# Seven products for eight in one block of gate and up columns, spread through the feed-forward

## The chip, the cores and the metric

The kernel runs on one core of a Trainium2 chip. The metric is the device time of one execution in microseconds (us), as the median of the runs. TensorE (PE) multiplies, VectorE (DVE) and ScalarE (ACT) work on tiles in the on-chip memories SBUF and PSUM, GpSimd (POOL) and SyncE (SP) here mostly issue DMAs.

## The reference

One block of a Conformer kind on 256 rows of width 1024 (feed-forward, mixer, feed-forward), then two post-norm attention layers; all in float32. The change touches the two feed-forwards only:

```python
D_MODEL, SEQ, D_FF = 1024, 256, 2816

def swiglu_ffn(x, w_gate, w_up, w_down):
    return (jax.nn.silu(x @ w_gate) * (x @ w_up)) @ w_down

x = x + 0.5 * swiglu_ffn(rmsnorm(x, ffn1_norm[l]), ffn1_w_gate[l], ffn1_w_up[l], ffn1_w_down[l])
x = x + hybrid_mixer(...)
x = x + 0.5 * swiglu_ffn(rmsnorm(x, ffn2_norm[l]), ffn2_w_gate[l], ffn2_w_up[l], ffn2_w_down[l])
...
```

## The kernel before

A float32 product is made of three float32r matmuls: both factors are split into a rounded part and a rest (`hi`, `lo`), and `half` adds `xh*whi`, `xl*whi` and `xh*wlo` in one PSUM bank. The 256 rows are two tiles t = 0, 1 of 128, kept transposed in `xT[t]` as eight k tiles of 128.

**Units.** Weights come in units of 512 KB (`unit_list`, in the order of use): two k tiles by 512 columns, or, for the last 256 columns, four k tiles. `load` issues a unit's DMA on SP into one of four `raw` buffers; `prefetch` splits it, the rounding `whi` on ACT (L198), the rest `wlo` on DVE (L199), into one of eight pairs of buffers (`N_W`, `AHEAD`). So the split of a unit waits until TensorE has released the unit eight places earlier, and a DMA until the split four places earlier has read its buffer.

**A feed-forward** (`ffn`) goes through six blocks of columns, j = 0 to 4 of 512 and j = 5 of 256 (`FFN_CH`). For each there is a chunk of gate units and one of up units; a chunk is 4 units, which tile t = 0 uses in turn and then t = 1, 48 matmuls of 512 columns in all. The first gate chunk of the first feed-forward has 8 units of half the size, of which both tiles use each at once (`first_chunk`, `first_x`). A gate chunk's sums go through ACT (`th`) and DVE (`a`), an up chunk's through DVE (`h`, then its transpose `hb`). The block of h is then brought into the layout of the next product by a trip through device memory (`regroup`): four DMAs `d<-hb` and one `hd<-d`, all issued by POOL in its order. When `hd` is back, `put_h` splits it on ACT and DVE (`hh`, `hl`, L240 and L241) into `hT`. `put_h` is entered in the order a fixed time after the trip (`DUE["ffn_T"]`, 7 us of an estimated clock), and pinned there: what follows on ACT and DVE waits if `hd` is late. Before the down product's second last pair all that is due is entered (`drain`).

**The down product** takes 11 units (k tiles 0,1 to 20,21, in this order) for each half of the 1024 columns; a unit's 12 matmuls are six for each tile.

Each engine runs its instructions in order. The order is written by the program's loops and the estimated clock, and by a scheduler that may move unpinned instructions.

Of the kernel before, what the change touches and what calls it, by code (L numbers as in the profile page):

```python
# [45 lines left out]

def unit_list():
# [39 lines left out]
    "ffn_T": 7.0,  # L87
# [28 lines left out]
class Kern:  # L116
    def __init__(self, ctx, tc, A):
# [11 lines left out]
        self.raw, self.W = {}, {}  # L129
# [57 lines left out]
    def prefetch(self, splits):  # L187
        nc = self.nc
        for _ in range(splits):
            if self.n_split < min(len(UNITS), self.used + AHEAD):  # L190
                self.load(self.n_split)
                i = self.n_split
                raw = self.raw.pop(i)
                nk, w = UNITS[i][2], UNITS[i][4]
                hi = self.wp.tile([P, UK * 512], F32R, name="whi", tag="whi", bufs=N_W)
                lo = self.wp.tile([P, UK * 512], F32R, name="wlo", tag="wlo", bufs=N_W)
                m = nk * w
                nc.scalar.copy(hi[:, :m], raw[:, :m])  # L198
                nc.vector.tensor_sub(lo[:, :m], raw[:, :m], hi[:, :m].bitcast(F32))  # L199
                self.W[i] = (hi[:, :m].rearrange("p (k n) -> p k n", k=nk),  # L200
                             lo[:, :m].rearrange("p (k n) -> p k n", k=nk))
                self.n_split += 1
        self.load(self.n_split + N_RAW - 2)

    def load(self, upto):
        while self.n_dma <= min(upto, len(UNITS) - 1):
            i = self.n_dma
            m = UNITS[i][2] * UNITS[i][4]
            raw = self.wp.tile([P, UK * 512], F32, name="raw", tag="raw", bufs=N_RAW)
            w = self.A["w"]  # L210
            self.nc.sync.dma_start(out=raw[:, :m], in_=bass.AP(
                tensor=w.tensor, offset=w.offset + self.off[i], ap=[[m, P], [1, m]]))
            self.raw[i] = raw
            self.n_dma += 1

# [162 lines left out]
    def ffn(self, u, gain, next_gain):  # L378
        nc, tc = self.nc, self.tc
        with tc.tile_pool(name="ffn", bufs=1, reuse_waits="tile") as pool:  # L380
# [13 lines left out]
            for j, (c0, w) in enumerate(FFN_CH):  # L394
                nu = KT * w // (UK * 512)
                ng = KT if u == 0 else nu
                a = [None, None]
                gen = self.first_chunk(u, ng, gain) if u == 0 else \
                    self.chunk(u, ng, gain if j == 0 else None)
                for t, acc in gen:  # L400
                    if j == 0:
# [844 lines left out]
```

## Time and profile before

| | us |
|---|---|
| median of 3 runs (719.29, 720.04, 1176.42) | 720.04 |
| the profiled execution | 717.48 |
| its span, first to last instruction | 715.7 |
| TensorE busy | 701.6 |
| VectorE busy | 491.4 |
| ScalarE busy | 368.8 |

The profiled execution's own time is 1.8 us above its span. Busy TensorE time counts overlapping matmuls once; how fast it goes is read from the distance between matmuls. The first feed-forward lies at about 8 to 188 us, the second at about 283 to 463 us.

### The profile page before, as it was taken

How to read it: one execution, taken by the hardware profiler on the slowest of the kernel's cores; microseconds unless marked ns; L12 is line 12 of the kernel's file. 1: busy time of each engine (PE TensorE's matmuls, PEld its weight loads, DVE VectorE, ACT ScalarE, POOL GpSimd, SP SyncE). 2: the span in 40 equal slices, each digit the busy share in tenths (PEclk: the TensorE clock that was granted, in tenths of full speed). 3: DMA queues.
4: the chain of work that ended last, by engine and by line, in shares of the span. 5: the costliest groups of instructions: out<-in, count | busy, mean ns of one | idle time of the engine just before them, and what ended most of it. 6: DMA issues, size and time to landing. Idle time of an engine off the chain costs nothing.

```text
span 715.7 us, 9843 instructions
## 1 busy us (share of the span) xinstructions
PE 701.6 (98%) x3594; PEld 590.0 (82%) x3594; DVE 491.4 (69%) x790; ACT 368.8 (52%) x552; POOL 62.2 (9%) x90
## 2 busy tenths in 40 slices
PE   8999999999999999999999999999999999999995
PEld 6788888888888778888888888888898888778984
DVE  5867765576547878655865576555456968997965
ACT  6664544364546646353544364555465635675820
POOL 0101110200002001011110200000300001000001
PEclk9999999999999999999999999999999999999998
DMA  8888566876744435558656867555672527543501
GB/s 257 311 313 301 209 217 212 302 229 221 254 151 145 178 115 172 194 197 290 208 209 220 293 229 228 175 192 174 206 253 77 159 83 230 195 123 114 177 1 59
DMA packets 42305, 140.87 MB, mean 197 GB/s; under 512 B 5512, under 2 KB 6672, under 8 KB 42128
## 3 DMA queue, kind: packets, MB, share of 16 engines
q1 hardware_dynamic: 37728, 127.23, 52.9%
q0 software_dynamic: 4096, 12.60, 5.0%
q8 instruction: 28, 0.46, 0.3%
q10 hardware_dynamic: 432, 0.41, 0.2%
q14 instruction: 21, 0.17, 0.1%
HBM read 133.39 MB, written 6.82 MB: 196 GB/s over the span
## 4 chain that ended last, share of the span: by engine, by line
PE 89%; DVE 4%; DMA 4%; ACT 2%; issue 1%; POOL 0%; SPq 0%; DVEq 0%; ACTq 0%; POOLq 0%
PE mm L165 80%; PE sc L165 5%; PE tr L180 3%; DMA raw<-in_w 1%; DVE wlo L199 1%; DMA rope<-in_rope 1%; PE tr L165 1%; DMA xin<-in_xT 1%; ACT whi L198 1%; DMA gain<-in_gain 0%; ACT s L452 0%; DVE sel L994 0%; DVE sel L1003 0%; ACT xh L323 0%; DVE s L543 0%
## 5 line engine op out<-in xcount | busy, mean ns | idle before, releaser
L199 DVE TENSOR_TENSOR wlo<-raw,whi 128x1024 fp32r<-128x1024 f32 (+3 forms) x236 | 274.3, 1177 | 83.0 <-ACT whi L198 73.4
L198 ACT CAST whi<-raw 128x1024 fp32r<-128x1024 f32 (+3 forms) x236 | 235.2, 1013 | 126.9 <-PE mm L165 65.7
L165 PE MATMUL mm<-whi,xh 128*128 128x512 f32 (+3 forms) x760 | 288.4, 380 | 1.9 <-ACT whi L198 1.9
L165 PE MATMUL mm<-wlo,xh 128*128 128x512 f32 (+3 forms) x760 | 283.4, 373 | 0.1
L165 PE MATMUL mm<-whi,xl 128*128 128x512 f32 (+3 forms) x760 | 283.4, 373 | 0.0
L165 PEld LDWEIGHTS mm<-whi,xh 128*128 128x128 f32 x760 | 143.2, 188 | 25.7 <-ACT whi L198 3.7
L165 PEld LDWEIGHTS mm<-wlo,xh 128*128 128x128 f32 x760 | 143.1, 188 | 25.5 <-DVE wlo L199 1.9
L165 PEld LDWEIGHTS mm<-whi,xl 128*128 128x128 f32 x760 | 143.3, 189 | 22.4 <-DVE xl L249 0.2
L165 PE MATMUL mm<-whi,hh 128*128 128x512 f32 x176 | 68.7, 390 | 0.0
L165 PE MATMUL mm<-whi,hl 128*128 128x512 f32 x176 | 68.5, 389 | 0.0
L165 PE MATMUL mm<-wlo,hh 128*128 128x512 f32 x176 | 68.5, 389 | 0.0
L241 DVE TENSOR_TENSOR hl<-hd,hh 128x512 fp32r<-128x512 f32 (+1 forms) x24 | 14.5, 644 | 59.4 <-ACT hh L240 59.4
L240 ACT CAST hh<-hd 128x512 fp32r<-128x512 f32 (+1 forms) x24 | 12.9, 583 | 67.0 <-DMA hd<-d 67.0
L285 POOL DMA_DIRECT2D d<-hb x48 | 26.5, 558 | 149.2 <-DVE hb L420 149.1
L165 PEld LDWEIGHTS mm<-wlo,hh 128*128 128x128 f32 x176 | 33.0, 188 | 6.9
L165 PEld LDWEIGHTS mm<-whi,hh 128*128 128x128 f32 x176 | 33.1, 188 | 6.8
L165 PEld LDWEIGHTS mm<-whi,hl 128*128 128x128 f32 x176 | 33.1, 188 | 6.7
L407 ACT ACTIVATE th<-mm,hr 128x512 f32<-128x512 f32 (+1 forms) x24 | 15.5, 648 | 19.9 <-PE mm L165 18.8
L452 ACT ACTIVATE s<-s,nmax 128x128 f32<-128x128 f32 (+1 forms) x48 | 21.3, 446 | 7.0 <-DVE nmax L450 7.0
L299 POOL TENSOR_TENSOR rs<-ms,mhalf 128x1 f32<-128x1 f32 x10 | 6.5, 652 | 169.7 <-DVE ms L312 169.7
L299 POOL TENSOR_TENSOR lr<-ve,mhalf 128x1 f32<-128x1 f32 x4 | 4.0, 991 | 167.6 <-DVE ve L651 167.6
L409 DVE SCALAR_TENSOR_TENSOR a<-th,mm 128x512 f32<-128x512 f32 (+1 forms) x24 | 15.1, 628 | 5.0 <-ACT th L407 5.0
(219 smaller groups left out, 598.6 us busy)
## 6 DMA issues: line engine op xcount, KB each, us to landing
raw<-in_w SPq DMA_DIRECT2D x208, 512.0 KB, 4.6
d<-hb POOLq DMA_DIRECT2D x40, 128.0 KB, 4.7
hd<-d POOLq DMA_DIRECT2D x10, 512.0 KB, 6.5
raw<-in_w SPq DMA_DIRECT2D x12, 344.0 KB, 3.4
raw<-in_w SPq DMA_DIRECT2D x8, 372.0 KB, 3.5
raw<-in_w SPq DMA_DIRECT2D x8, 256.0 KB, 4.4
x<-in_x SPq DMA_DIRECT2D x2, 512.0 KB, 6.6
B<-in_bias SPq DMA_DIRECT2D x1, 1024.0 KB, 5.5
```

Source lines behind the costliest of these rows:

```text
L165: self.nc.tensor.matmul(out, a, b, start=start, stop=stop)
L180: self.nc.tensor.transpose(out, a, self.ident[:p, :p])
L198: nc.scalar.copy(hi[:, :m], raw[:, :m])
L199: nc.vector.tensor_sub(lo[:, :m], raw[:, :m], hi[:, :m].bitcast(F32))
L240: i = nc.scalar.copy(hi, src)
L241: j = nc.vector.tensor_sub(lo, src, hi.bitcast(F32))
L285: self.nc.gpsimd.dma_start(out=d[a].rearrange("b i m -> i b m"), in_=src[32 * a:32 * a + 32])
L299: self.nc.gpsimd.tensor_tensor(out, a, self.mhalf[:, 0:1].to_broadcast(list(a.shape)), op=ALU.pow)
L407: nc.scalar.activation(th[:, :w], acc[:, :w], AF.Tanh, scale=hr[t])
L409: nc.vector.scalar_tensor_tensor(a[t][:, :w], th[:, :w], 1.0, acc[:, :w], op0=ALU.add, op1=ALU.mult)
L452: nc.scalar.activation(s[:, h, :], s[:, h, :], AF.Exp, bias=m[:, h:h + 1], accum_out=l[:, col + h:col + h + 1])
```

## The change

In each feed-forward the block j = 4 (`SB`) is taken out of the chunks. Its product, 256 rows by 1024 by (512 gate and 512 up columns), is cut in halves along all three: A11, A12 are `xT[0]`'s k tiles 0 to 3 and 4 to 7, A21, A22 those of `xT[1]`; B11, B21 are the two k halves of the gate columns, B12, B22 of the up columns. Seven products of two units (12 matmuls each) and sums of them give the four quarters. The weight sums grow in place: `sum` is B11 for P1, then B12 is added for P5, B22 for P6, B21 for P4; `sum3` is B12 + B22 for P7; P2 and P3 take B21 and B22 as they are. Each addition is a DMA that POOL issues and that adds what it reads to what stands in the buffer (`accum_op`). The sums of x are made on DVE (`whole`, `sum_of`, line 480 and on), split, and kept in the part of `hT` that the blocks 3 and 4 use later. Results are added up on DVE and ACT in four tiles `T4`. The products stand between the other chunks in the order `UP`; `put_h` is entered 12 us after a trip for 7; `DOWN_K` sets the order of the down units; `hb` has one buffer for two, `a` two for three.

```diff
+SB = 4
+UP = [("gate", 0), ("up", 0), ("gate", 1), "P1", ("up", 1), "P5", ("gate", 2), "P6", ("up", 2), "P7",
+      ("gate", 5), ("up", 5), "P2", ("gate", 3), "P4", "P3", ("up", 3)]
+DOWN_K = [0, 2, 4, 6, 8, 10, 20, 12, 14, 16, 18]
...
+SOURCE = {"P1": "sum", "P5": "sum", "P6": "sum", "P4": "sum", "P7": "sum3", "P2": "raw", "P3": "raw"}
...
-    "ffn_T": 7.0,
+    "ffn_T": 12.0,
...
-                nc.scalar.copy(hi[:, :m], raw[:, :m])
-                nc.vector.tensor_sub(lo[:, :m], raw[:, :m], hi[:, :m].bitcast(F32))
+                a = nc.scalar.copy(hi[:, :m], raw[:, :m])
+                b = nc.vector.tensor_sub(lo[:, :m], raw[:, :m], hi[:, :m].bitcast(F32))
+                if i in RECIPE:
+                    self.pin(a), self.pin(b)
...
+                for fn in self.events.pop(self.n_split, ()):
+                    fn()
...
+    def fetch(self, dst, i, add=False):
+
+        m, w = UNITS[i][2] * UNITS[i][4], self.A["w"]
+        src = bass.AP(tensor=w.tensor, offset=w.offset + self.off[i], ap=[[m, P], [1, m]])
+        if add:
+            self.nc.gpsimd.dma_start(out=dst[:, :m], in_=src, accum_op=ALU.add)
+        else:
+            self.nc.sync.dma_start(out=dst[:, :m], in_=src)
+
+    def plan(self, f):
+
+        def at(what, n, key, block, add=True):
+            def fn():
+                for g in range(2):
+                    self.fetch(self.kept[key, g], AT[f, block, g], add)
+            self.events.setdefault(AT[f, what, 1] + 1 + n, []).append(fn)
+        at("P1", 2, "sum", "P5")
+        at("P5", 1, "sum3", "P5", False)
+        at("P5", 2, "sum", "P6")
+        at("P6", 1, "sum3", "P6")
+        at("P6", 2, "sum", "P2")
+
+    def prod(self, acc, lhs, i):
+
+        xh, xl = lhs
+        for g in range(2):
+            if i + g not in self.W:
+                self.prefetch(i + g + 1 - self.n_split)
+            hi, lo = self.W[i + g]
+            for k in range(2):
+                kk = 2 * g + k
+                self.mm(acc, xh[:, kk, :], hi[:, k, :], kk == 0, False, 1)
+                self.mm(acc, xl[:, kk, :], hi[:, k, :], False, False, 1)
+                self.mm(acc, xh[:, kk, :], lo[:, k, :], False, kk == 3, 1)
+            self.pump()
+            self.done(i + g + 1)
+            self.prefetch(1)
...
+            def whole(k, t, y):
+                nc.vector.tensor_add(v4(T4[k]), quad(0, t, y), quad(1, t, y))
...
+            def sum_of(which, out, a, b, op):
+                nc.vector.tensor_tensor(T4[out], T4[a], T4[b], op=op)
+                self.split_psum(*SS[which], v4(T4[out]))
...
+                acc = self.bank("sc")
+                self.prod(acc, lhs, u)
+                tt = nc.vector.tensor_tensor
+                if what == "P1":
+                    nc.scalar.copy(T4["s"], acc)
+                elif what == "P5":
+                    nc.scalar.copy(T4["q"], acc)
+                elif what == "P6":
+                    tt(T4["m"], T4["s"], acc, op=ALU.add)
+                    tt(T4["r"], T4["q"], T4["m"], op=ALU.subtract)
+                elif what == "P7":
+                    tt(T4["m"], T4["m"], acc, op=ALU.add)
+                    tt(T4["q"], T4["q"], T4["m"], op=ALU.subtract)
+                else:
+                    k = {"P2": "s", "P4": "m", "P3": "r"}[what]
+                    tt(T4[k], T4[k], acc, op=ALU.add)
...
+            for what in UP:
+                if what in SOURCE:
+                    product(what)
+                    u += 2
+                    if what == "P3":
+                        hb = new_hb()
+                        for t, (x1, x2) in enumerate(("sr", "mq")):
+                            gate(t, T4[x1], 512, T4[x1])
+                            up(t, T4[x2], 512, hb, T4[x1])
+                        trip(SB, 4, hb)
+                    continue
...
-                    if n == 0 and i == nd - 2:
+                    if n == 0 and i == nd - 4:
                         self.drain()
```

Over the whole program TensorE has 24 matmuls fewer (2 times 12), DVE 50 instructions more, ACT 24, POOL 16 (the adding DMAs, 8 in each feed-forward); the number of SP's DMAs is the same. Outside the two feed-forwards the order on DVE, ACT, POOL and SP is as before.

VectorE in the first gate chunk, where the k tiles of x are split (`xl0` and `xl1` are the rests of the tiles t = 0 and 1) between the weight splits `wlo`. Before:

```order
L199 TENSOR_TENSOR wlo_180<-raw_93,whi_179 128x512
...
L324 SCALAR_TENSOR_TENSOR xl1_148<-xin_84,gain_72,xh1_147 128x128
L199 TENSOR_TENSOR wlo_196<-raw_96,whi_195 128x512
L324 SCALAR_TENSOR_TENSOR xl0_146<-xin_84,gain_72,xh0_145 128x128
...
L199 TENSOR_TENSOR wlo_212<-raw_163,whi_211 128x512
...
L199 TENSOR_TENSOR wlo_228<-raw_183,whi_227 128x512
```

Now, the same place:

```order
L221 TENSOR_TENSOR wlo_185<-raw_93,whi_184 128x512
...
L480 TENSOR_TENSOR ts_168<-xh0_145,xl0_146 128x512
L221 TENSOR_TENSOR wlo_201<-raw_96,whi_200 128x512
L399 SCALAR_TENSOR_TENSOR xl0_146<-xin_84,gain_72,xh0_145 128x128
...
L480 TENSOR_TENSOR tq_170<-xh1_147,xl1_148 128x512
L221 TENSOR_TENSOR wlo_217<-raw_163,whi_216 128x512
```

Two additions of whole quarters of x, `ts` and `tq`, now stand ahead of the split of the fifth half unit (`wlo_212` before, `wlo_217` now).

GpSimd in the first feed-forward, from the first trip on. Before, only trips follow each other:

```order
L285 DMA d_404<-hb_322 32x4x256 x4
L286 DMA hd_403<-d_404 128x4x256
L285 DMA d_578<-hb_496 32x4x256 x4
L286 DMA hd_577<-d_578 128x4x256
L285 DMA d_753<-hb_671 32x4x256 x4
```

Now:

```order
L360 DMA d_421<-hb_327 32x4x256 x4
L258 DMA sum_409<-in_w 128x1024 x2
L361 DMA hd_420<-d_421 128x4x256
L258 DMA sum3_167<-in_w 128x1024 x2
L258 DMA sum_409<-in_w 128x1024 x2
L360 DMA d_622<-hb_542 32x4x256 x4
L258 DMA sum_409<-in_w 128x1024
L361 DMA hd_621<-d_622 128x4x256
```

The additions for P5 stand ahead of the first trip's `hd`, and one of those for P4 ahead of the second trip's.

VectorE around the first `put_h` of the first feed-forward (`hl0`, `hl1`). Before, the splits up to the fourth unit of gate block 2 stand ahead of it:

```order
L199 TENSOR_TENSOR wlo_592<-raw_526,whi_591 128x1024
L199 TENSOR_TENSOR wlo_610<-raw_548,whi_609 128x1024
L241 TENSOR_TENSOR hl0_81<-hd_403,hh0_80 128x512
L241 TENSOR_TENSOR hl1_83<-hd_403,hh1_82 128x512
L418 SCALAR_TENSOR_TENSOR h_534<-a_449,qr0_300,mm_497 128x512
L199 TENSOR_TENSOR wlo_633<-raw_566,whi_632 128x1024
```

Now:

```order
L221 TENSOR_TENSOR wlo_551<-raw_500,whi_550 128x1024
L221 TENSOR_TENSOR wlo_567<-raw_523,whi_566 128x1024
L316 TENSOR_TENSOR hl0_81<-hd_420,hh0_80 128x512
L316 TENSOR_TENSOR hl1_83<-hd_420,hh1_82 128x512
L537 SCALAR_TENSOR_TENSOR h_578<-a_469,qr0_305,mm_543 128x512
L538 STREAM_TRANSPOSE hb_542<-h_578 128x4x128
L221 TENSOR_TENSOR wlo_589<-sum_409,whi_588 128x1024
L221 TENSOR_TENSOR wlo_607<-sum_409,whi_606 128x1024
```

The last split ahead of it is now that of the up block 1's fourth unit; P5's two splits (`wlo<-sum`) stand behind it, and gate block 2 behind those.

## Rows read from the trace of the kernel before

**Rows 1.** The page: span, and each engine's busy time.

```profile
span 715.7 us, 9843 instructions
...
PE 701.6 (98%) x3594; PEld 590.0 (82%) x3594; DVE 491.4 (69%) x790; ACT 368.8 (52%) x552; POOL 62.2 (9%) x90
```

**Rows 2.** The chain that ended last: start us, us, what.

```profile
12.73 5.02 DMA raw<-in_w
17.85 1.05 ACT whi L198
...
20.20 143.38 PE mm L165 x674
...
282.96 148.95 PE mm L165 x702
...
432.78 28.59 PE mm L165 x126
```

**Rows 3.** Groups by form, 283 to 430 us: count | busy us, mean ns.

```profile
L199 DVE TENSOR_TENSOR wlo<-raw,whi 128x1024 fp32r<-128x1024 f32 x54 | 64.8, 1218 | 13.7 <-ACT whi L198 12.0 <-PE mm L165 0.4
...
L198 ACT CAST whi<-raw 128x1024 fp32r<-128x1024 f32 x54 | 55.3, 1051 | 27.0 <-DMA raw<-in_w 13.6 <-PE mm L165 5.8 <-issue 4.5
...
L418 DVE SCALAR_TENSOR_TENSOR h<-a,qr,mm 128x512 f32<-128x512 f32 x10 | 7.4, 743 | 2.1 <-PE mm L165 2.1
...
L241 DVE TENSOR_TENSOR hl<-hd,hh 128x512 fp32r<-128x512 f32 x10 | 6.5, 689 | 31.0 <-ACT hh L240 31.0
L240 ACT CAST hh<-hd 128x512 fp32r<-128x512 f32 x10 | 5.7, 619 | 34.1 <-DMA hd<-d 34.1
```

**Rows 4.** Busy time by stretch: stretch, engines' busy us, clock, DMA share, GB/s.

```profile
40.00:52.00 12.00, 12.00 (x55) 9.94 (x54) 7.02 (x8) 6.85 (x9) 0.77 (x1) 1.00 0.93 343
62.00:84.00 22.00, 22.00 (x99) 18.22 (x98) 14.21 (x16) 9.86 (x13) 2.68 (x6) 1.00 0.67 222
...
316.00:338.00 22.00, 22.00 (x99) 18.23 (x98) 14.65 (x16) 10.43 (x12) 2.94 (x5) 1.00 0.69 231
```

**Rows 5.** VectorE's timeline in the first 14 us: start us, us, what.

```profile
9.49 0.69 DVE L199 TENSOR_TENSOR wlo<-raw,whi 128x512 fp32r<-128x512 f32 x1
10.10 1.76 DVE L324 SCALAR_TENSOR_TENSOR xl<-xin,gain,xh 128x128 fp32r<-128x128 f32 x6
12.01 0.69 DVE L199 TENSOR_TENSOR wlo<-raw,whi 128x512 fp32r<-128x512 f32 x1 [0.16 <-ACT whi L198]
```

**Rows 6.** TensorE's timeline at the second chunk's first matmul.

```profile
18.95 0.50 PE L165 MATMUL mm<-whi,xh 128*128 128x512 f32 x1 [1.18 <-ACT whi L198]
```

**Rows 7.** DMA issues, 30 to 50 us: count, KB each, median us to landing.

```profile
raw<-in_w SPq DMA_DIRECT2D x10, 512.0 KB, 5.7
...
hd<-d POOLq DMA_DIRECT2D x1, 512.0 KB, 7.2
```

**Rows 8.** VectorE's timeline around the first return trip, 45 to 54 us.

```profile
50.76 1.23 DVE L199 TENSOR_TENSOR wlo<-raw,whi 128x1024 fp32r<-128x1024 f32 x1 [3.00 <-ACT whi L198]
51.90 1.29 DVE L241 TENSOR_TENSOR hl<-hd,hh 128x512 fp32r<-128x512 f32 x2
```

**Rows 9.** GpSimd's timeline, the first trip's DMA issues.

```profile
34.17 2.39 POOL L285 DMA_DIRECT2D d<-hb  x4 [9.65 <-DVE hb L420]
41.81 0.77 POOL L286 DMA_DIRECT2D hd<-d  x1 [5.25 <-DMA d<-hb]
```

**Rows 10.** GpSimd's timeline, a trip in the second feed-forward.

```profile
326.60 2.18 POOL L285 DMA_DIRECT2D d<-hb  x4 [17.16 <-DVE hb L420]
334.05 0.76 POOL L286 DMA_DIRECT2D hd<-d  x1 [5.28 <-DMA d<-hb]
```

**Rows 11.** VectorE's timeline at the end of that trip.

```profile
323.80 0.75 DVE L418 SCALAR_TENSOR_TENSOR h<-a,qr,mm 128x512 f32<-128x512 f32 x1
...
325.60 0.70 DVE L420 STREAM_TRANSPOSE hb<-h 128x512 f32<-128x512 f32 x1
...
341.74 1.29 DVE L241 TENSOR_TENSOR hl<-hd,hh 128x512 fp32r<-128x512 f32 x2 [7.05 <-ACT hh L240]
```

More of the change, by code (lines that the diff above doesn't have):

```diff
@@ L56, in ffn @@
     def ffn(i):
-        for c0, w in FFN_CH:
-            block(f"gate{i}", c0, w, n=1 if i == 1 and c0 == 0 else None)
-            block(f"up{i}", c0, w)
+        for what in UP:
+            if what in SOURCE:
+                m, k = BLOCK.get(what, ("gate", 0))
+                for g in range(2):
+                    RECIPE[len(u)] = (what, g, i)
+                    AT[i, what, g] = len(u)
+                    u.append((f"{m}{i}", k + 2 * g, 2, 512 * SB, 512 if what in BLOCK else 0))
+            else:
+                m, j = what
+                block(f"{m}{i}", *FFN_CH[j], n=1 if i == 1 and what == ("gate", 0) else None)
         for n in range(2):
-            block(f"down{i}", 512 * n, 512, 0, FT)
+            for k in DOWN_K:
+                u.append((f"down{i}", k, 2, 512 * n, 512))
     ffn(1)
@@ L207, in load @@
             i = self.n_dma
[L208 to L213, printed above, removed]
-            self.n_dma += 1
+            self.n_dma += 1
+            if i in RECIPE:
+                what, g, f = RECIPE[i]
+                if what == "P1":
+                    if g == 0:
+                        sums = self.fpool.tile([P, 2, UK * 512], F32, name="sum", tag="xin")
+                        self.kept.update((("sum", k), sums[:, k, :]) for k in range(2))
+                    self.fetch(self.kept["sum", g], i)
+                if SOURCE[what] != "raw":
+                    continue
@@ L393, in ffn @@
                 self.start(gain)
-            for j, (c0, w) in enumerate(FFN_CH):
-                nu = KT * w // (UK * 512)
[L396 to L401, printed above, removed]
+            f = 1 if u == 0 else 2
+            self.fpool = pool
+            s3 = pool.tile([P, 2, UK * 512], F32, name="sum3")
@@ new lines, in ffn @@
+            self.kept = {("sum3", g): s3[:, g, :] for g in range(2)}
+            SS = {"1234"[i]: tuple(hT[i // 2][c][:, 12 + 4 * (i % 2):16 + 4 * (i % 2), :] for c in range(2))
+                  for i in range(4)}
+            T4 = {k: pool.tile([P, 512], F32, name="t" + k) for k in "smqr"}
+            self.plan(f)
+            quad = lambda c, t, y: self.xT[t][c][:, 4 * y:4 * y + 4, :].bitcast(F32)
+            def whole(k, t, y):
+                nc.vector.tensor_add(v4(T4[k]), quad(0, t, y), quad(1, t, y))
@@ new lines, in quad2, with gate @@
+            def quad2(t, y):
+                return tuple(d[:, 4 * y:4 * y + 4, :] for d in self.xT[t])
+            a = [None, None]
+            def gate(t, g, w, out=None):
+                th = pool.tile([P, 512], F32, name="th", bufs=2)
+                nc.scalar.activation(th[:, :w], g[:, :w], AF.Tanh, scale=hr[t])
+                if out is None:
+                    out = a[t] = pool.tile([P, 512], F32, name="a", bufs=2)
+                nc.vector.scalar_tensor_tensor(out[:, :w], th[:, :w], 1.0, g[:, :w], op0=ALU.add, op1=ALU.mult)
```

88 lines of the change are left out of this document (66 added, 22 removed).

## The prediction

> **What bounds the kernel now.** I read the page's busy times first: TensorE is busy 98% of the span, VectorE 69%, ScalarE 52% [rows 1]. Busy matmuls overlap, so the second view is the chain that ended last. In both feed-forwards it is TensorE without a break: from 20.2 to 163.6 us in the first, from 283.0 to 431.9 us in the second [rows 2]. Its last row gives the price of a matmul of 512 columns, 28.59 us / 126 = 0.227 us, and so of a unit's twelve 2.72 us. A stretch without a gap says that all splits came in time, not how early; that is read from the others: over 44 us of chunks VectorE is busy 28.9 us (66%), ScalarE 20.3 us (46%), and the DMA engines 67 to 69%, but 93% at 343 GB/s between 40 and 52 us [rows 4]. The first feed-forward starts from empty buffers; the second finds its eight pairs full.
>
> **What is taken away.** Seven products of 12 matmuls stand for 96, so 12 matmuls go in each feed-forward: 24 x 0.227 = 5.4 us off TensorE's chain. Each matmul loads its own weights before as now, so nothing else changes in its price. That is the most that this change gives while TensorE has no gap, 0.8%.
>
> **What VectorE and ScalarE get.** For each feed-forward 14 splits stand for 8: six more at 1.218 us on VectorE and at 1.051 us on ScalarE [rows 3]. VectorE also gets 4 additions of quarters of x, 4 further sums, 4 rests and 7 additions of results, 19 instructions of 128 x 512, which I price as the nearest row of that size, 0.689 us [rows 3]: 7.3 + 13.1 = 20.4 us. ScalarE gets 6.3 us and six copies of at most 0.7 us, some 10 us. The chunks' stretch is 44 units, 119.8 us, and becomes 117.1 us. VectorE's 66% of it is 78.6 us and becomes 99 us, 85%; ScalarE goes from 46% to 56%. Both stay below TensorE, so on the average I cost this at nothing; the cover is a lead of eight units in the buffers. Where it is gone, the 20.4 us are on the path.
>
> **The start of the first feed-forward: +1.0 us (0 to 1.3).** Here is no lead. Before, the first 1024-column unit's DMA ran from 12.73 to 17.75 us, and its split led to TensorE's gap of 1.18 us at 18.95 [rows 2, 6]. The DMA started then because its buffer is that of the fifth half unit, whose rest VectorE finished at 12.01 + 0.69 = 12.70 us [rows 5]. Two additions (`ts`, `tq`) now stand ahead of that rest. 2 x 0.65 us less the 0.16 us in which VectorE waited there [rows 5] is 1.1 us; the DMA, the split and TensorE's restart move with it. I take 1.0, since the matmuls ahead of the gap also end later and the order behind it is a little better. If the DMA lands faster for starting later, it is 0.
>
> **P5 in the first feed-forward: +3.1 us (0 to 6).** TensorE reaches P5 at 18.95 + 1.0 + 8 units of up 0 and gate 1 (21.8) + P1 (2.7) + up 1 (10.9) = 55.4 us; its third matmul, the first that needs a rest, 0.45 us later. VectorE has the first `put_h` ahead of P5's splits. Before, its `hl` came at 51.90 us, after POOL's `hd` DMA at 41.81 with 7.2 us to landing [rows 7 to 9]. With the shift and the added sums the trip starts about 1.5 us later, so `hd` is issued at 43.3 and would land at 50.5. But the two additions for P5 are queued ahead of it on the same queue: 1.05 MB, at 343 GB/s [rows 4] another 3.1 us, so 53.6. From there ScalarE's `hh` (0.6, less than `hl`), two `hl` (1.3) [rows 8], one `h` and its transpose (0.74, 0.70) [rows 3, 11], and P5's first rest (1.22): 58.1 us against 55.8, a stall of 2.3 us. Then VectorE needs 7.5 us for P5's second rest, gate block 2's four and an `h` and transpose, TensorE 6.8 us: 0.8 more. Bounds: 0, if the additions don't delay `hd` (55.0 against 55.8); 6, if they take twice the bytes' time. I take the sum of the middle, 3.1, since 40 to 52 us is where the DMA engines were already full.
>
> **P6, P7 and the second feed-forward: 0 (to 3).** Before, no adding DMA is in the trace. Its bounds are a plain DMA's 5.7 to 7.2 us for 512 KB [rows 7], and twice that; a pair in flight is then 9 to 15 us. In the second feed-forward the splits of P5 may start some 14 us ahead of their use (eight units, of which two are short), and between two adding steps lie 13.6 us of TensorE's work, so a pair of 9 to 15 us is covered. The eight more loads of 512 KB, 4.2 MB, take 12 us of full DMA rate at 343 GB/s; the engines idle for 31 to 33% of 117 us, 37 us. Entering `put_h` five units of the clock later takes back the wait that ended at `hl` with 7.05 us [rows 11], so the trip too is covered there.
>
> **The down product: +0.4 us (0 to 4).** Block 3 is now the last of the chunks and stands at place 7 of the down order: TensorE wants it 7 x 2.72 = 19.1 us after up 3 ends. A trip took from `h` at 323.80 over the `d` DMAs at 326.60 and `hd` at 334.05 to the end of `hl` at 343.03: 19.2 us [rows 10, 11]. The first tile's `hl` ends 0.6 us earlier. So this is even; I take 0.2 us in each feed-forward, and 2 if block 4's trip, just ahead, delays it.
>
> **Sum.** -5.4 + 1.0 + 3.1 + 0 + 0.4 = -0.9 us. The profiled execution, 717.5 us (span 715.7 and 1.8 around it), would be 716.6 us. The median of the runs is 720.0, 2.6 us above it; there I forecast **719.1 us**. A measurement of this kernel tells about 2%, 14.4 us, from no change, so this is no change.
>
> **The rivals.**
>
> *All is hidden.* The additions share the DMA engines without delaying `hd`, and the start costs nothing: -5.4 to -3, about 715.5 us. For it: before, `hl` waited up to 7 us without a gap on TensorE [rows 11]. Against it: in the first feed-forward the DMA engines were full just when the first additions come [rows 4].
>
> *Adding DMAs move their bytes twice* (the buffer is read and written). The pair ahead of `hd` then takes 6.2 us: P5's stall is 5.4 + 0.8. For P6 the four additions of `sum3` and `sum` count 4.2 MB, 12.2 us after P5's second rest at 62.5, with the split's 2.3 us 77; TensorE wants it at 75.5 or so: +2. One us more for the second feed-forward's trips. -5.4 + 1.0 + 6.2 + 2 + 1 + 0.4 = +5.2, so 725 us.
> The Trainium skill, "Collectives: The Full Stack", section "The bandwidth ceiling: the fold count and why AG ≠ RS ≠ AR", says that an adding transfer has two source reads where a copy has one, and that this halves its rate. By that page this rival would be the likeliest; no run before shows an adding DMA, so it stays a rival.
>
> *The adding DMAs are slow, and the kernel is slower.* One place decides: P6, whose splits wait for an addition that may only start when P5's splits have read `sum`, 13.6 us of TensorE's work earlier. ScalarE and VectorE have P6's splits in a fixed place, so all later splits wait too. A pair of X us beyond the 13.6 us stalls TensorE by about X - 13.6 in each feed-forward. From X = 23 us it costs 18.8 us, less the 4.4 us that the rest of the sum leaves without P5's stall: over 2% slower. At X = 30 us: 33 - 4 + 4 at P5 = 753 us. For it: nothing in the trace bounds an addition from above. Against it: 23 us is three times the 7.2 us of a plain DMA of half the size, under 50 GB/s.
>
> **How the numbers follow.** My forecast, with stalls that leave -3 to +2, has a chance of 0.50; all hidden 0.22; bytes twice 0.20 (722 to 728); slow additions 0.07; that the scheduler or the queues do something that costs or gives more in another way 0.01. The range from 714 to 728 holds the first three and leaves out the slow additions and the edges. Slower by over 2% (734.4) is the slow case alone, 0.07; faster by over 2% (705.6) has no case above 0.01, since only 5.4 us are taken away; within 2% 0.92.
>
> **What would show it.** TensorE's matmuls number 24 fewer, still 0.227 us apart. Right if the chain has one short gap near 20 us, one of 2 to 4 us near 56 us that ends at a rest of `sum`, and none between 290 and 400 us. The start is wrong if TensorE's gap still ends at 18.95. The DMA table shows 16 adding DMAs with their landing time: 6 to 10 us is my case, over 20 the slow one. Block 3's `hl` should end just before the eighth down unit. The forecast is wrong if VectorE, at 85%, falls behind on its own where no DMA is late.

## The result, and the profile after

The changed kernel takes 739.48 us (median of four runs, 735.59 to 744.78) against 719.66 for the kernel before: ratio 1.0285, 95% interval 1.0204 to 1.0366, slower. One disturbed run of the kernel before (1176.42) is left out. The profiled execution is the 744.78 one, so its losses are on the large side.

The page after, beside [rows 1]: TensorE has 24 matmuls fewer and is busy 96% for 98%.

```profile
span 743.0 us, 9879 instructions
...
PE 709.9 (96%) x3570; PEld 591.8 (80%) x3570; DVE 528.1 (71%) x840; ACT 387.0 (52%) x576; POOL 77.0 (10%) x106
```

The span is 27.3 us longer, and all of it is lost in the two feed-forwards, before the second half of each down product: the first transposes there, which end TensorE's row in the chain, stand at 181.3 and 459.3 us for 163.6 and 431.9. So the first feed-forward costs 17.7 us more and the second 9.6. Where [rows 2] had TensorE from end to end, the chain that ended last now runs through trips, splits and raw loads (start us, us, what):

```profile
44.93 12.10 DMA hd<-d
61.44 3.48 DVE wlo L221 x3
...
134.50 7.08 DMA raw<-in_w
...
154.82 5.56 DMA raw<-in_w
160.48 1.05 ACT whi L220
163.44 17.85 PE mm L185 x65
...
398.14 4.24 DMA hd<-d
416.52 6.10 DMA raw<-in_w
428.15 5.69 DMA d<-hb
434.49 6.78 DMA hd<-d
441.96 17.31 PE mm L185 x66
460.14 28.58 PE mm L185 x126
```

TensorE's timeline gives the places; in brackets the idle time ahead of a matmul and what ended it. These are all rows of 0.6 us or more in the two feed-forwards:

```profile
61.57 0.80 PE L185 MATMUL sc<-wlo,hh 128*128 128x512 f32 x1 [3.72 <-DVE wlo L221]
112.75 0.50 PE L185 MATMUL mm<-wlo,xh 128*128 128x512 f32 x1 [1.36 <-DVE wlo L221]
133.51 0.50 PE L185 MATMUL mm<-whi,hh 128*128 128x512 f32 x1 [0.66 <-ACT whi L220]
162.10 0.50 PE L185 MATMUL mm<-whi,hh 128*128 128x512 f32 x1 [4.70 <-ACT hh L315]
163.44 0.80 PE L185 MATMUL mm<-whi,hl 128*128 128x512 f32 x1 [0.84 <-DVE hl L316]
404.10 0.50 PE L185 MATMUL mm<-whi,xh 128*128 128x512 f32 x1 [2.02 <-ACT whi L220]
441.96 0.80 PE L185 MATMUL mm<-whi,hh 128*128 128x512 f32 x1 [5.41 <-ACT hh L315]
```

The first is P5, those at 162.1, 163.4 and 441.96 are block 3 in the two down products; only P5 had been forecast as a gap of this size. And the matmuls behind such a gap are slow. From the same timeline, behind the gap at 404.10 and 405.36:

```profile
405.96 0.63 PE L185 MATMUL mm<-whi,xh 128*128 128x512 f32 x1
406.38 0.63 PE L185 MATMUL mm<-whi,xl 128*128 128x512 f32 x1
406.81 0.63 PE L185 MATMUL mm<-wlo,xh 128*128 128x512 f32 x1
...
408.73 0.39 PE L185 MATMUL mm<-whi,xl 128*128 128x512 f32 x1
408.96 0.39 PE L185 MATMUL mm<-wlo,xh 128*128 128x512 f32 x1
```

They start 0.43 us apart, the 1.2 GHz level, and then again 0.227, the 2.4 GHz level. The view by stretches shows the same as a granted clock under 1 behind P5 and behind block 3 (columns as in [rows 4]: stretch, length, busy us of PE, PEld, DVE, ACT, POOL, clock, DMA share, GB/s):

```profile
41.00:52.00 11.00, 11.00 (x50) 9.12 (x49) 7.50 (x7) 6.83 (x8) 4.38 (x5) 1.00 1.01 281
52.00:63.00 11.00, 7.28 (x29) 5.68 (x28) 5.25 (x7) 5.13 (x6) 0.85 (x1) 0.88 1.02 305
63.00:74.00 11.00, 11.00 (x41) 8.94 (x40) 6.24 (x8) 3.40 (x5) 3.10 (x5) 0.81 0.97 249
...
162.00:173.00 11.00, 10.06 (x31) 7.83 (x32) 5.82 (x7) 4.56 (x6) 0.00 (x0) 0.69 0.65 220
```

With these the profiled execution can be balanced. "Slow" is the sum, over the matmuls of 512 columns in the timeline, of what they stand further apart than 0.227 us beyond the gaps, less the 0.5 us that the kernel before has by the same sum.

| us | first feed-forward | second |
|---|---|---|
| 12 matmuls fewer | -2.7 | -2.7 |
| P5 | 3.7 | 0 |
| short block, 112.75 and 404 | 1.4 | 2.5 |
| block 3 (and 0.7 at the down product's first matmul) | 6.2 | 5.4 |
| slow matmuls behind the gaps | 6.7 | 4.0 |
| sum | 15.3 | 9.2 |
| measured | 17.7 | 9.6 |

Most of the 2.4 us that are missing in the first column belongs to the start: the second `th` stands at 27.23 us for 24.80 before.

### The profile page after: what moved, and what is told of

It reads as the page before. It is cut to its first block, busy times and chain, and to the rows that moved or that the text cites. A ratio compares the mean times of both kernels' runs of the same rounds, so it can differ in the third digit from the quotient of the medians.

```text
span 743.0 us, 9879 instructions
## 1 busy us (share of the span) xinstructions
PE 709.9 (96%) x3570; PEld 591.8 (80%) x3570; DVE 528.1 (71%) x840; ACT 387.0 (52%) x576; POOL 77.0 (10%) x106
## 4 chain that ended last, share of the span: by engine, by line
PE 55%; DMA 19%; DVE 14%; issue 6%; ACT 3%; POOL 2%; SPq 0%; DVEq 0%; POOLq 0%; ACTq 0%
PE mm L185 45%; DMA hd<-d 8%; DMA raw<-in_w 7%; DVE wlo L221 6%; PE sc L185 5%; PE tr L200 3%; DMA d<-hb 3%; ACT whi L220 2%; POOL d L360 1%; DMA x<-in_x 1%; DVE h L537 1%; DVE hb L538 1%; DVE hl L316 1%; DMA xin<-in_xT 1%; PE tr L185 1%
## 5 line engine op out<-in xcount | busy, mean ns | idle before, releaser
L221 DVE TENSOR_TENSOR wlo<-raw,whi 128x1024 fp32r<-128x1024 f32 (+3 forms) x228 | 265.0, 1179 | 86.9 <-ACT whi L220 79.5
L220 ACT CAST whi<-raw 128x1024 fp32r<-128x1024 f32 (+3 forms) x228 | 227.3, 1011 | 145.3 <-PE mm L185 83.8
L185 PE MATMUL mm<-whi,xh 128*128 128x512 f32 (+3 forms) x696 | 264.6, 380 | 3.0 <-ACT whi L220 2.9
L185 PE MATMUL mm<-wlo,xh 128*128 128x512 f32 (+3 forms) x696 | 259.9, 374 | 3.0 <-DVE wlo L221 2.9
L185 PE MATMUL mm<-whi,xl 128*128 128x512 f32 (+3 forms) x696 | 259.1, 373 | 0.0
L185 PEld LDWEIGHTS mm<-wlo,xh 128*128 128x128 f32 x696 | 131.5, 189 | 28.3 <-DVE wlo L221 6.9
L185 PEld LDWEIGHTS mm<-whi,xh 128*128 128x128 f32 x696 | 132.0, 190 | 25.0 <-ACT whi L220 5.3
L185 PEld LDWEIGHTS mm<-whi,xl 128*128 128x128 f32 x696 | 131.8, 189 | 20.0 <-DVE xl L324 0.2
L185 PEld LDWEIGHTS mm<-whi,hh 128*128 128x128 f32 x176 | 34.2, 194 | 19.2 <-ACT hh L315 10.9
L316 DVE TENSOR_TENSOR hl<-hd,hh 128x512 fp32r<-128x512 f32 (+1 forms) x24 | 14.4, 643 | 33.9 <-ACT hh L315 33.9
L221 DVE TENSOR_TENSOR wlo<-sum,whi 128x1024 fp32r<-128x1024 f32 x20 | 23.6, 1215 | 4.3 <-ACT whi L220 4.3
L220 ACT CAST whi<-sum 128x1024 fp32r<-128x1024 f32 x20 | 20.5, 1048 | 9.8 <-DMA sum<-in_w 6.8
```

What stands on the lines that cost most here:

```text
L185: self.nc.tensor.matmul(out, a, b, start=start, stop=stop)
L220: a = nc.scalar.copy(hi[:, :m], raw[:, :m])
L221: b = nc.vector.tensor_sub(lo[:, :m], raw[:, :m], hi[:, :m].bitcast(F32))
L316: j = nc.vector.tensor_sub(lo, src, hi.bitcast(F32))
```

## The experiments

All edits are to the changed kernel unless another is named. The table has what was measured; gaps are TensorE's idle time by its timeline in the profiled execution, "short" is the place near 113 us and 400 us, and a star marks a gap that stands at the chunk behind P5.

| run | median us | ratio to before, interval | P5 | short, 1st / 2nd | block 3, 1st / 2nd |
|---|---|---|---|---|---|
| changed kernel | 739.48 | 1.0285 (1.0204 to 1.0366) | 3.7 | 1.4 / 2.5 | 5.5 / 5.4 |
| block 3 last | 725.10 | 1.0073 (1.0045 to 1.0101) | 2.6 | 3.4 / 1.3 | 0.8 / 0.7 |
| trips entered late | 732.45 | 1.0172 (1.0141 to 1.0204) | 2.5 | 0.5 / 0 | 4.9 / 3.9 |
| plain DMAs | 734.84 | 1.0192 (1.0144 to 1.0240) | 0.3 | 2.2 / 0 | 6.2 / 5.5 |
| no products | 722.04 | 1.0035 (1.0010 to 1.0059) | 0 | 0 / 0 | 0 / 2.5 |
| both edits | 720.06 | 1.0012 (0.9997 to 1.0028) | 3.3 | 0 / 0 | 0.7 / 0 |
| own loads | 738.54 | 1.0267 (1.0233 to 1.0302) | 0 | 1.9 / 1.6 | 4.3 / 5.2 |
| products later | 726.03 | 1.0105 (1.0087 to 1.0122) | 1.8 | 1.7 / 0 | 0.7 / 0 |
| second only | 715.22 | 0.9953 (0.9941 to 0.9966) | 0 | 0 / 0 | 0 / 0 |
| own loads, no sums | 739.34 | 1.0301 (1.0261 to 1.0341) | 0 | 4.0 / 1.8 | 5.4 / 5.7 |
| block 4 late, plain | 723.16 | 1.0057 (1.0035 to 1.0078) | 0 | 0 / 0 | 0 / 2.3 |
| three splits ahead | 750.35 | 1.0442 (1.0421 to 1.0462) | 0.9 | 3.0 / 3.1 | 7.4 / 6.7 |
| both edits, ahead | 717.98 | 0.9995 (0.9976 to 1.0013) | 1.7* | 0 / 0 | 1.4 / 0 |
| no sums, late entry | 728.77 | 1.0153 (1.0132 to 1.0174) | 0 | 0 / 0 | 4.8 / 2.6 |
| unpinned | 742.31 | 1.0344 (1.0318 to 1.0370) | 2.9* | 3.8 / 0 | 6.5 / 7.2 |
| unpinned, both edits | 722.16 | 1.0057 (1.0037 to 1.0076) | 3.0* | 0.5 / 0 | 2.8 / 0 |
| no products, both edits | 718.18 | 0.9993 (0.9984 to 1.0002) | 0 | 0 / 0 | 0 / 0 |

### First question: the adding DMAs, or block 3's trip?

**Block 3 last.**

```diff
-DOWN_K = [0, 2, 4, 6, 8, 10, 20, 12, 14, 16, 18]
+DOWN_K = [0, 2, 4, 6, 8, 10, 20, 16, 18, 12, 14]
...
-                    if n == 0 and i == nd - 4:
+                    if n == 0 and i == nd - 2:
```

> Blocks 3 and 4 change places in the order of the down product, so TensorE wants block 3 two units (5.4 us) later. Theory A (the late trip of block 3): the gaps of 5.5 us in the first and 5.4 us in the second feed-forward fall to under 1 us each, and the low granted clock behind them (0.69 and 0.73 over 11 us, some 3 us each) goes with them: 739.5 - 16 = 723 us, 720 to 728. Theory B (the adding DMAs hold up all other transfers): the `hd` of both blocks is late by the same cause, the gap moves to block 4 or to the raw weights, and the time is 734 us or more.

Theory A by the time and the gaps: 14.4 us come back, and 5 us on TensorE in each feed-forward. Block 3 is as late as it was (`hh` 22.9 and 24.4 us after up 3's last matmul in the two feed-forwards, for 22.3 and 23.9); it is only wanted 5.4 us later.

**Trips entered late.**

```diff
-    "ffn_T": 12.0,
+    "ffn_T": 18.0,
```

> The `put_h` of each trip is entered 18 us of the planner's clock after the trip instead of 12, nothing else. Theory A': the stalls at P5 in the first feed-forward (3.7 us) and at 404 us in the second (2.6 us) come from splits queued behind an `hh` or `hl` that waits for its `hd`; both fall under 1 us, with the low clock behind them (some 3 and 2 us), and the two gaps at the down product stay: 739.5 - 11 = 728 us, 725 to 733. Theory B (the adding DMAs themselves are late): P5 still waits for its `sum` DMAs or for raw weights, and the time is 736 us or more.

The gap at 404 us is gone, the one near 113 falls from 1.4 to 0.5, P5's from 3.7 to 2.5 (two gaps, 0.87 for a `whi` and 1.64 for a `wlo`); block 3's stay. So the wait at 404 was ScalarE held by the short block's `hh`. This is the row in the changed kernel that says so, with two splits right behind it (the timeline of ScalarE):

```profile
402.39 0.71 ACT L315 CAST hh<-hd 128x256 fp32r<-128x256 f32 x2 [6.37 <-DMA hd<-d]
403.01 1.99 ACT L220 CAST whi<-raw 128x1024 fp32r<-128x1024 f32 x2
```

At P5 2.5 us are left, more than theory A' forecast. They end at splits of `sum`, but the late entry has not freed these splits: ScalarE now has `hh` ahead of both, and waits for `hd`, although the two additions for P5 had landed at 48.18 and 52.41 us:

```profile
55.14 1.14 ACT L315 CAST hh<-hd 128x512 fp32r<-128x512 f32 x2 [8.99 <-DMA hd<-d]
56.19 1.99 ACT L220 CAST whi<-sum 128x1024 fp32r<-128x1024 f32 x2
```

**Plain DMAs.**

```diff
-            self.nc.gpsimd.dma_start(out=dst[:, :m], in_=src, accum_op=ALU.add)
+            self.nc.gpsimd.dma_start(out=dst[:, :m], in_=src)
```

> The sixteen adding DMAs lose their addition: the same bytes on the same queue at the same places overwrite `sum` and `sum3`, so the weight sums of the products are left out. Theory B (the addition's double traffic is what costs): their median landing falls from 9.2 to about 5.7 us, the DMA share between 41 and 63 us from 1.01 to about 0.85, P5's stall falls under 1 us, and the gaps at the down product shrink too: 728 us or less. Theory A: P5's stall shrinks as well (the first `hd` lands some 4 us sooner), 3 to 7 us in all, but both gaps of over 5 us at the down product stay: 732 to 737 us.

P5's stall is the addition's price: 3.7 us fall to 0.3, and the first `hd` takes 9.2 us to land for 12.1. Block 3's gaps do not shrink, so theory A holds there. GpSimd's queue (packets, MB, share of 16 engines' span) in the kernel before, then the same and the issue table (count, KB each, median us to landing) of the changed kernel:

```profile
q0 software_dynamic: 4096, 12.60, 5.0%
```

```profile
q0 software_dynamic: 6400, 20.98, 11.6%
```
```profile
sum<-in_w POOLq DMA_DIRECT2D x16, 512.0 KB, 9.2
```

and with plain DMAs in the same places:

```profile
q0 software_dynamic: 6400, 20.98, 8.8%
```
```profile
sum<-in_w POOLq DMA_DIRECT2D x16, 512.0 KB, 5.7
```

**No products.** Block 4 becomes gate and up chunks; the orders, one `hb`, two `a` and the 12 us stay.

```diff
-UP = [("gate", 0), ("up", 0), ("gate", 1), "P1", ("up", 1), "P5", ("gate", 2), "P6", ("up", 2), "P7",
-      ("gate", 5), ("up", 5), "P2", ("gate", 3), "P4", "P3", ("up", 3)]
+UP = [("gate", 0), ("up", 0), ("gate", 1), ("up", 1), ("gate", 2), ("up", 2),
+      ("gate", 5), ("up", 5), ("gate", 4), ("up", 4), ("gate", 3), ("up", 3)]
```

> No Strassen products, no sums of x or of weights: block 4 is again plain gate and up chunks, but the order of the blocks (3 last), the order of the down product, one `hb`, two `a` and the 12 us stay as in the changed kernel. Theory A (the order alone makes block 3 late): a gap of 4 to 6 us at block 3 in each down product with its low clock behind it, no gap at P5's place: 720 + 16 = 736 us, 729 to 738. Theory B (the added DMAs and splits make it late): no gap over 1 us, 719 to 722 us.

Mostly theory B, and against what I thought by then: the order alone leaves nothing in the first feed-forward and 2.5 us in the second, not 4 to 6 in both. The products do make block 3 late, but not by their adding DMAs. How, the two timelines show. Without products the down product starts at 129.99 us, and on VectorE `h` and the transpose of the second tile follow at once (VectorE, then GpSimd's issues, then ScalarE):

```profile
131.67 0.74 DVE L536 SCALAR_TENSOR_TENSOR h<-a,qr,mm 128x512 f32<-128x512 f32 x1
...
133.46 0.70 DVE L537 STREAM_TRANSPOSE hb<-h 128x512 f32<-128x512 f32 x1
...
134.46 2.19 POOL L360 DMA_DIRECT2D d<-hb  x4 [14.93 <-DVE hb L537]
141.95 0.76 POOL L361 DMA_DIRECT2D hd<-d  x1 [5.30 <-ACT whi L220]
...
146.34 1.14 ACT L315 CAST hh<-hd 128x512 fp32r<-128x512 f32 x2 [1.72 <-DMA hd<-d]
```

In the changed kernel the first four matmuls of the down product (from 133.51 us on) stand in TensorE's order ahead of the last twenty of up 3, which therefore ends at 139.1 us:

```profile
138.88 0.39 PE L185 MATMUL mm<-wlo,xh 128*128 128x512 f32 x1
139.10 0.39 PE L185 MATMUL mm<-wlo,hh 128*128 128x512 f32 x1
```

The second tile's `h` follows 1.6 us later, as soon as without products (1.7), but splits that wait stand around it:

```profile
139.59 1.23 DVE L221 TENSOR_TENSOR wlo<-raw,whi 128x1024 fp32r<-128x1024 f32 x1 [1.80 <-ACT whi L220]
140.73 0.74 DVE L537 SCALAR_TENSOR_TENSOR h<-a,qr,mm 128x512 f32<-128x512 f32 x1
142.76 1.23 DVE L221 TENSOR_TENSOR wlo<-raw,whi 128x1024 fp32r<-128x1024 f32 x1 [1.29 <-ACT whi L220]
143.91 1.29 DVE L538 STREAM_TRANSPOSE hb<-h 128x512 f32<-128x512 f32 x2
...
145.50 2.19 POOL L360 DMA_DIRECT2D d<-hb  x4 [3.52 <-DVE hb L538]
153.40 0.76 POOL L361 DMA_DIRECT2D hd<-d  x1 [5.71 <-DMA d<-hb]
...
161.43 1.14 ACT L315 CAST hh<-hd 128x512 fp32r<-128x512 f32 x2
```

The transposes end 6.1 us after up 3 (145.20) for 4.2, and issue to `hh` takes 15.9 us for 11.9. Of these 4.0 us, 2.3 are not the trip's: `hd` had landed at 159.14, and `hh` stood on ScalarE behind a split that waited for a raw load, the last row below. In the second feed-forward the transposes end 8.9 us after up 3 for 4.9, `h` itself comes 5.1 us after it, and issue to `hh` is 14.8 us for about 15.7. The `wlo` above wait for `whi`, and `whi` for raw loads:

```profile
138.50 1.05 ACT L220 CAST whi<-raw 128x1024 fp32r<-128x1024 f32 x1 [3.81 <-DMA raw<-in_w]
141.68 1.05 ACT L220 CAST whi<-raw 128x1024 fp32r<-128x1024 f32 x1 [2.13 <-DMA raw<-in_w]
...
160.48 1.04 ACT L220 CAST whi<-raw 128x1024 fp32r<-128x1024 f32 x1 [3.03 <-DMA raw<-in_w]
```

Without products ScalarE waited there for TensorE to free a buffer, which means that the buffers were full. The lead, the units split ahead of their use, can also be counted: when up 3 ends, five and four down units have their rests in the run without products (first and second feed-forward), and two and two in the changed kernel. So the question became: what empties the buffers?

### Second question: what empties the split buffers

**Own loads.** No adding DMA, no `sum`: each product reads a quarter of the block through the raw buffers.

```diff
-SOURCE = {"P1": "sum", "P5": "sum", "P6": "sum", "P4": "sum", "P7": "sum3", "P2": "raw", "P3": "raw"}
+SOURCE = {k: "raw" for k in ("P1", "P5", "P6", "P4", "P7", "P2", "P3")}
+LOADS = {"P3": "P6", "P4": "P2", "P7": "P5"}
...
-            self.plan(f)
```

> Against the changed kernel: every product loads one quarter of a weight block of its own through the ordinary raw buffers, and no adding DMA, no `sum` and no `sum3` exist; the weight sums are left out of the products. The fourteen splits, the sums of x and the additions of results stay, and SP issues 14 loads for the products. Theory A2 (the six more splits and the 19 instructions on VectorE empty the lead): the gaps at block 3 in the down product stay at 3 us or more in both feed-forwards, 728 to 736 us. Theory B2 (the weight sums, whose splits wait for additions that wait for earlier splits, empty it): the gaps fall to what the order alone gave (0 and 2.3 us), 717 to 723 us. P5's stall is under 0.5 us by both.

Theory A2, if a little above its time: without any adding DMA the kernel is as slow as the changed one, and block 3 as late.

**Own loads, no sums.** The products take quarters of x for sums, and the result additions go too.

```diff
-                    for i in range(4):
-                        self.later(1.0 + 4.0 * i, lambda i=i: sums(i))
...
-                    tt(T4["m"], T4["s"], acc, op=ALU.add)
-                    tt(T4["r"], T4["q"], T4["m"], op=ALU.subtract)
+                    nc.scalar.copy(T4["m"], acc)
```

> As the run in which the products load blocks of their own, and the sums of x (8 additions and 4 splits) and the 7 additions of results are left out too; two copies on ScalarE take results instead. What stays is seven products with fourteen splits. Theory V (the 19 instructions on VectorE make block 3's `h`, transposes and splits late): the gaps at block 3 fall to at most 1 us in the first and 2.5 us in the second feed-forward, 717 to 723 us. Theory L (the fourteen loads and splits for units of half the length empty the lead): the gaps stay at 3 us or more in both, 727 to 738 us.

Theory L (1 us above its range): gaps of 5.4 and 5.7 us. VectorE's added sums are not the cause.

**Block 4 late, plain.** The control for the two trips that stand close together. The edit is to the run without products.

```diff
-      ("gate", 5), ("up", 5), ("gate", 4), ("up", 4), ("gate", 3), ("up", 3)]
+      ("gate", 5), ("up", 5), ("gate", 4), ("gate", 3), ("up", 4), ("up", 3)]
```

> No products, the same order and down product as the run without products, except that gate 3 is computed between gate 4 and up 4 (with four buffers for `a`, and without the buffers of the sums), so that block 4's trip starts 10.9 us ahead of block 3's, as in the changed kernel, and not 21.8. Theory O (two trips close together on one `hb`, POOL's queue and the DMA engines make block 3 late): a gap of 3 us or more at block 3 in both down products, 726 to 734 us. Theory L or V (the products' work ahead of it does): as the run without products, none in the first and at most 2.5 us in the second feed-forward, 719 to 724 us.

Theory O falls: 0 and 2.3 us, as without products.

**Three splits ahead.** While a product runs, the code stands only one unit ahead with the splits.

```diff
+                if what == ("up", 0):
+                    self.prefetch(3)
...
-                    self.prefetch(1)
+                    if n or i >= 3:
+                        self.prefetch(1)
```

> Against the changed kernel only the place of the splits moves: behind up 0 of each feed-forward three splits more are written ahead, and the first three splits of the down product are left to later, so that in the chunks a split stands three units further ahead in the code (4 units instead of 1 while a product runs), with the same buffers. Theory P (what empties the buffers is that a product's splits are written only one unit of 1.36 us ahead, behind `th` and `hh` that wait, so that ScalarE, VectorE and then the DMA queue stand still): the gaps near 113 and 404 us go, ScalarE waits less for `th` ahead of a `whi<-sum`, block 3's gaps fall to at most 1.5 us in the first and 2.5 us in the second feed-forward, and the time is 720 to 728 us. Theory L' (fourteen loads and splits are simply too many for the DMA engines and VectorE): block 3's gaps stay at 4 us or more, 734 us or more.

Theory P falls, and by much: 750.35 us, above both. The earlier splits move all of ScalarE's row, P6 now stalls 1.7 us as well, and `hh` of the short block holds ScalarE for 7.88 us

```profile
125.83 0.71 ACT L315 CAST hh<-hd 128x256 fp32r<-128x256 f32 x2 [7.88 <-DMA hd<-d]
```

just ahead of the last chunks.

**Unpinned.**

```diff
-                if i in RECIPE:
-                    self.pin(a), self.pin(b)
```

> Against the changed kernel only the calls of `pin` on the products' splits are taken out, so that the scheduler may move them, and it puts them and the splits behind them ahead of `th` and `hh` that wait (the two splits behind P4 now ahead of gate 3's first `th`). Theory Q (pinned splits stand behind `th` and `hh`, and all later splits behind them): the waits of ScalarE for `th` and `hh` no longer hold splits, the gaps near 113 and 404 us go, and block 3's gaps fall to at most 2.5 us, 720 to 729 us. Theory L: the buffers are empty before block 3 all the same and its gaps stay at 4 us or more, 734 us or more.

Theory Q falls too; the same `hh` waits 7.78 us here. Both runs name the waiting `hh`, which the next takes away.

**No sums, late entry.** The run without sums, with 18 us.

> The run with loads of their own and no sums, and `put_h` entered 18 us after the trip instead of 12. Theory H (the pinned `hh` of the short block, for which ScalarE waited 7.0 us near 115 us, holds the splits behind it and so empties the buffers just ahead of block 3): with the later entry ScalarE is never held by `hh` in the chunks, the gaps at 118 and 399 us go, and block 3's gaps fall from 5.4 and 5.7 to at most 2 us, 719 to 726 us. Theory L (fourteen loads and splits are too many by themselves): block 3's gaps stay at 4 us or more, 729 us or more.

Half each. The gaps in the short block's place are gone, the time falls by 10.6 us, and in the second feed-forward block 3's gap falls to 2.6 us, what the order alone gives: there theory H is right. In the first it stays at 4.8 us, with ScalarE still waiting for raw loads, though the DMA engines are busy only 70 to 92% between 53 and 141 us. Some 2.9 of the 4.8 us are such a wait just ahead of `hh`: `hd` had landed at 147.21 us, and `hh` ran at 150.13.

### Third question: is there a version that gains?

**Both edits** (block 3 last, 18 us), and the same with the products one chunk later, with three splits ahead, and unpinned:

> Both edits at once: blocks 3 and 4 change places in the down product, and `put_h` is entered 18 us after the trip. If the two losses are separate, what is left is 5.4 us saved less the start (0.5), P5 (2.5), 109 us (0.5 to 1), the down product (0.5 to 1.5) and some 1.5 of lower clock, so 719 to 722 us, no change against the kernel before. If the late entry only moves the waiting, the first edit's gaps come back (hd later at the down product) and it is 725 us or more.

The two losses are separate: 739.5 becomes 720.1, no change against the kernel before. What is left is P5 in the first feed-forward, 3.3 us and a clock of 0.74 behind it (60 to 71 us). It is again `hh` ahead of P5's splits on ScalarE, 9.79 us for `hd`.

> As the run with both edits, and the products P1, P5, P6, P7 and P2 each stand one chunk later (after up 1, gate 2, up 2, the short block, and gate 3). Theory: P5 stalls because its additions fall into 41 to 63 us, where the DMA engines are still filling the lead and are full; 11 us later they are not, so P5's stall falls under 1 us: 716 to 719 us. Rival: the additions fill the DMA engines wherever they stand, P5 stalls by 2 us or more in its new place or block 3 is late again, and the time is 721 us or more.

The rival: P5 stalls 1.8 us in its new place, P6 1.6 and the short block 1.7. So it is not one bad place in the first feed-forward; that it is the amount of work there fits, but is not shown apart from this.

> The products in both feed-forwards with all three edits: block 3 last in the down product, `put_h` entered 18 us after the trip, and the splits written three units further ahead. If the edits add up, what is left beside the 5.4 us saved is the start (0 to 0.5) and at P5 of the first feed-forward 1 to 3 us with its lower clock: 714 to 718 us, ratio 0.993 to 0.999. Rival: in the first feed-forward the splits ahead only bring the loads earlier into the stretch where the DMA engines are full, and P5 stalls as long as before, 719 us or more.

By the median the top of the range, but the interval holds 1: no gain shown. With `hh` out of the way the splits ahead do no harm, against 11 us without. P5's splits now stand ahead of the first `hh`, and P5 does not stall; the chunk behind it does, with ScalarE waiting 5.56 us for a raw load.

> Products in both feed-forwards, splits unpinned, block 3 last in the down product, `put_h` entered 18 us after the trip. If the pins are what costs beside the order of the blocks, only the start and a part of P5 in the first feed-forward are left: 714 to 717 us, ratio 0.993 to 0.998. Rival: as the same run with pins, 719 us or more.

The rival, with the same gap at the chunk behind P5 (3.0 us): pins are not what costs.

**Second only.** Both edits, products in the second feed-forward alone.

```diff
-            for what in UP:
+            for what in (PLAIN if f == 1 else UP):
```

> The run with both edits, but with the products in the second feed-forward alone; the first computes block 4 by plain gate and up chunks in the order of the run without products. If the losses left are those of the first feed-forward (its start from empty buffers and P5), this one keeps 2.7 us of the saved matmuls and loses 0.3 to 1.5 in the second: 716.5 to 718.5 us, ratio 0.997 to 1.000. Rival: the second feed-forward loses its saving too, 720 us or more.

715.22 us, 0.5% faster than the kernel before, and below the range of either theory, since the second feed-forward loses nothing: TensorE has no gap over 0.2 us in it, and from 283.95 to its first transposes at 430.15 us it takes 146.2 us, where the row of [rows 2] had 149.0.

**No products, both edits**, its control:

> No products in either feed-forward, with block 3 last in the down product and `put_h` entered 18 us after the trip: what is left of the run with products in the second feed-forward when its products are taken out too. If that run's 3.6 us (0.47%) are the twelve matmuls saved there (2.7 us), this one is the kernel before within its noise: 717.5 to 719.5 us, ratio 0.999 to 1.002, no gap over 0.5 us at either down product. If they come of the new order and the later entry, it is 714.5 to 716.5 us.

718.18 us, the kernel before within its noise. The gain of the run above, 3.0 us to this one, is that of the twelve matmuls (2.7).

## Why the prediction was wrong

**Matmuls taken away** (-5.4): right. 24 fewer, 0.227 us apart where the clock is whole, and the second feed-forward alone gave its half.

**The start** (+1.0, 0 to 1.3): about 2 us, above its bound. TensorE's restart moved by 0.65 us (19.60 for 18.95), inside the bounds; the four small gaps behind it (0.17 to 0.29 us each) had not been counted. Of the 2.4 us by which the second `th` comes later, some 1 us is not placed.

**P5** (+3.1): 3.7 us, from the right cause. `hd` was issued at 44.93 (43.3 forecast) and took 12.1 us where 10.3 had been summed. The price of an adding DMA was the wrong value inside the right bounds. GpSimd's queue took 5.0% of 16 engines' 715.7 us for 4096 packets before, 0.14 us each; the 2304 added packets took 0.35 us each as additions and 0.20 as plain DMAs, a factor of 1.75. So the rival that moves the bytes twice was near in its price. It was wrong on the place and the time: it expected 725, and by the run with plain DMAs the addition explains some 4.6 of the 19.8 us lost (739.48 less 734.84 and less 719.66). The Trainium skill, "Collectives: The Full Stack", section "The bandwidth ceiling: the fold count and why AG ≠ RS ≠ AR", puts the factor at two for the adding step of collectives; the trace agrees about that far, with 1.75 by packet time and 1.6 by the median landing (9.2 for 5.7). The rival of slow additions has the right size of time and the wrong cause: it needed 23 us or more for P6's pair, which took 10.9 us in the first feed-forward (62.05 to 72.94), and P6 did not stall.

**P6, P7 and the second feed-forward** (0 to 3): 2.5 us at 404, inside the range, by another mechanism than those I weighed. "Entering `put_h` five units of the clock later ... so the trip too is covered there" is the step that failed: 12 us was still too early for the short block's trip, and in this kernel what stands behind that `hh` are splits that TensorE is about to need. The first feed-forward lost 1.4 us in the same place, which was not in the sum.

**The down product** (+0.4, 0 to 4): this is the step that failed and decides. It cost 5.5 and 5.4 us of idle time, 11 for 0.4. When TensorE wants block 3 was right (19.2 us after the down product's start at 417.35). When it comes was counted from `h` to the end of `hl`, as if `h` began when up 3 ends and nothing that waits stood between. In the second feed-forward `h` began 5.1 us after up 3's end and the transposes were over after 8.9. In the first they were over after 6.1, the trip took longer, and `hh` stood 2.3 us behind a split although `hd` was there; the chain that ended last goes through that split's raw load. Each time it was splits that waited for raw loads.

That the forecast left these waits out rested in turn on "the cover is a lead of eight units in the buffers", read from the average (VectorE at 85%): VectorE's work did come out as summed (528.1 for 491.4 us, 36.7 for 40.8 forecast) and did no harm by itself, but the lead was not there: when up 3 ended two down units had their rests in each feed-forward, where the kernel before had five. Without the adding DMAs, without the sums as well, or without the pins block 3 stays late, and the order without products costs nothing in the first feed-forward. What remains, by elimination and not by a run of its own, is the fourteen loads and splits for units of half the length. The count agrees: two and two units with plain DMAs or own loads, two and three without sums. With the late entry as well it is two and five: in the second feed-forward the products empty the buffers only together with a `hh` that is entered too early.

**The clock** was not in the sum at all: 6.7 and 4.0 us of matmuls at half speed behind the gaps, more than any other loss in the first feed-forward and less only than block 3's in the second. The 8.0 us of gaps in the second feed-forward cost 12.0.

Of the signs that the forecast named, P5's gap, the additions' landing (9.2 us) and the stretch without a gap from 290 to 400 us came true. The one that failed is block 3's `hl` just ahead of the eighth down unit, and it is the one that 11 us hung on.

What stays open is why the buffers do not fill again in the first feed-forward even with late entries and no sums. That four raw buffers limit it (in that run the queue of raw loads waited 51 us, between 60 and 125 us, for VectorE's `wlo` to free one) fits, but was not tried.

## What to carry to other kernels

A lead in buffers is no cover that can be read off an average: count the loads and splits per microsecond of the bottleneck's work at the place itself, and ask what stands behind each in-order wait there. Count a trip from the end of the matmuls that feed it, with what is queued ahead of its first and its last step, not from the start of the first. And check in the engine's order what stands ahead of the matmuls that feed it. Where the matmul engine has been without a gap, price each new gap with the slow matmuls behind it, and put a block whose trip is long where it is wanted last.

## What the runs showed of the hardware

- An adding DMA of 512 KB landed after 9.2 us (median) where a plain one in the same place took 5.7, and its packets took 0.35 us of an engine for 0.20. Between 41 and 63 us the DMA engines were full at 281 to 305 GB/s, less than the 343 GB/s at 0.93 before [rows 4] and the 369 at 1.00 with plain DMAs (41 to 52 us).
- Behind gaps of 2 to 5 us the matmuls of 512 columns stood 0.43 us apart, with granted clocks of 0.69 to 0.93 in stretches of 11 us, and then went back to 0.227. Behind the gap of 1.36 us at 112.75 the clock stayed at 1.00 (107 to 118 us). In all the stalls cost half of their length again, or more: 11.3 us of gaps and 6.7 of slow matmuls in the first feed-forward, 8.0 and 4.0 in the second.
